# Two early stores moved beside the last row maximum, and six one-element memsets behind it

## The chip, the cores and the metric

The kernel runs on one core of a Trainium2 chip. It uses three engines: SyncE issues the transfers (DMA), VectorE and GpSimd compute. The metric is device time in microseconds (us).

The **span** of a profile goes from the first to the last instruction of the kernel's own program. The **time** is some 1.7 to 2.0 us longer.

## The reference

```python
x = np.random.randn(8192, 8192).astype(np.float32)
return np.linalg.norm(x, ord=np.inf, axis=1)      # the largest |x| of each row
```

It is 268 MB read once and 32 KB written.

## The kernel before

SyncE issues all loads into a ring of buffers (`ring`), VectorE takes the absolute maximum of each piece, and GpSimd combines the maxima of rows that were cut. The first 23 loads of two rows per partition are all alike; the last 18 rows per partition come in 25 loads that get smaller towards the end, so that VectorE and the stream end nearly together. A load waits for its room in the ring, and a maximum waits for the sixteen semaphore increments of its load (the trace of the kernel before has 816 landings, sixteen for each of 48 loads and 3 stores).

```python
def load(self, at, w, src):
    ins = self.nc.sync.dma_start(out=self.ring[:, at : at + w], in_=src)
    ins.then_inc(self.sems[i % SEMS], 16)
    ...
def reduce(self, pairs):
    for k, (dst, src) in enumerate(pairs):
        ins = self.nc.vector.tensor_reduce(out=dst, in_=src, axis=X, op=max, apply_absolute_value=True)
        ...
        ins.wait_op(self.sems[i % SEMS], 16 * (i // SEMS + 1), "sem-ge")     # the first of the load's pieces
    self.last.append(ins.ins)
```

The end of the kernel has three stores: `res_big` (the 46 results per partition of the big loads), the first 16 of the tail's 18 columns, and its last two. SyncE issues the first two right behind the last load; the third waits for the last maximum.

```python
tc.declare_fence(done.ins, group="loads")
nc.sync.dma_start(out=out[:split]..., in_=res_big...)                              # 128 x 184 B
nc.sync.dma_start(out=out_tail[:, : ROWS - 2], in_=res_tail[:, : ROWS - 2])        # 128 x 64 B
seen = nc.sync.keepalive_nop(...)      # waits for GpSimd's last column
last = nc.sync.dma_start(out=out_tail[:, ROWS - 2 :], in_=res_tail[:, ROWS - 2 :]) # 128 x 8 B
```

## Time and profile before

| | before |
|---|---|
| time, median of 3 runs | 629.49 us (629.48 to 629.49) |
| time of the profiled execution | 629.77 us |
| its span | 627.8 us |
| VectorE busy | 551.9 us, 88% |
| DMA, mean | 428 GB/s |

The lines of the page, of the chain, of the timeline and of the traffic that carry the argument stand in the prediction. SyncE's own waits in the last 20 us of the kernel before (who waited, for whom, us in total, times, longest) complete them:

```profile
SPq L218 <- POOL res_tail L202: 13.6, 1, 13.6
SPq L222 <- DVE res_tail L106: 1.3, 1, 1.3
SPq L248 <- DMA out_dram<-res_tail: 1.0, 1, 1.0
```

SyncE has nothing to do from the early stores' issue at 610.5 us to 624.2 us; then it waits for the last maximum, issues the last store, and waits for its landing. So it has room for two issues beside the last maximum.

### The profile page before, as it was taken

The page shows a single profiled execution, that of the slowest core. Times are in us where ns is not written, and L with a number is a line of the kernel's source. Part 1 is how long each engine was busy: PE and PEld are TensorE (multiplying, and loading weights), DVE is VectorE, ACT ScalarE, POOL GpSimd, SP SyncE. Part 2 cuts the span into 40 slices and gives each one's busy share as a digit, 9 for nine tenths or more (in the row PEclk, how much of TensorE's full clock was granted, in tenths as well). Part 3 has the DMA queues.
Part 4 walks back from the last instruction along what each step waited for, and adds up shares of the span by engine and source line. Part 5 has one row for each costly group of instructions (what it writes and reads, how often), then busy time and mean ns, then how long its engine had stood idle before and what let it go on. Part 6 is the DMA issues. An engine that isn't in the chain of part 4 may idle for free.

```text
span 627.8 us, 164 instructions
## 1 busy us (share of the span) xinstructions
DVE 551.9 (88%) x56; POOL 2.9 (0%) x13
## 2 busy tenths in 40 slices
DVE  0588988889988889888898888998889899999998
POOL 0000000000000000000000000000000000000000
DMA  9999999999999999999999999999999999999997
GB/s 401 413 455 409 459 405 463 405 463 401 468 401 468 401 468 401 468 401 468 401 468 401 468 401 468 401 468 401 468 390 435 452 419 438 426 422 431 427 422 284
DMA packets 7344, 268.47 MB, mean 428 GB/s; under 512 B 1200, under 2 KB 1200, under 8 KB 1968
## 3 DMA queue, kind: packets, MB, share of 16 engines
q1 hardware_dynamic: 7344, 268.47, 99.2%
HBM read 268.44 MB, written 0.03 MB: 428 GB/s over the span
## 4 chain that ended last, share of the span: by engine, by line
DMA 59%; DVE 40%; issue 0%; SPq 0%
DMA ring<-in_x_dram 59%; DVE res_big L106 22%; DVE parts L106 10%; DVE res_tail L106 8%; SPq L88 0%
## 5 line engine op out<-in xcount | busy, mean ns | idle before, releaser
L106 DVE TENSOR_REDUCE res_big<-ring 128x2 f32<-128x16384 f32 x23 | 396.1, 17220 | 69.3 <-DMA ring<-in_x_dram 69.3
L106 DVE TENSOR_REDUCE res_tail<-ring 128x1 f32<-128x8192 f32 (+1 forms) x10 | 79.0, 7945 | 2.6 <-DMA ring<-in_x_dram 2.6
L106 DVE TENSOR_REDUCE parts<-ring 128x1 f32<-128x3520 f32 (+17 forms) x19 | 69.8, 3738 | 1.7 <-DMA ring<-in_x_dram 1.7
L106 DVE TENSOR_REDUCE ring<-ring 128x1 f32<-128x1984 f32 (+3 forms) x4 | 7.7, 1982 | 0.0
L202 POOL TENSOR_SCALAR res_tail<-parts 128x1 f32<-128x1 f32 x8 | 2.3, 291 | 614.0 <-DVE parts L106 614.0
L202 POOL TENSOR_SCALAR parts<-parts 128x1 f32<-128x1 f32 x1 | 0.4, 357 | 7.0 <-DVE parts L106 7.0
L237 POOL MEMSET const-bfloat16-1.0<- 128x1 bf16 x1 | 0.1, 103 | 0.0
L237 POOL MEMSET const-uint8-127<- 128x1 uint8 x1 | 0.1, 102 | 0.0
L237 POOL MEMSET const-float32-0.0<- 128x1 f32 x1 | 0.1, 99 | 0.2 <-issue 0.2
L237 POOL MEMSET const-float32-1.0<- 128x1 f32 x1 | 0.1, 99 | 0.0
## 6 DMA issues: line engine op xcount, KB each, us to landing
ring<-in_x_dram SPq DMA_DIRECT2D x3, 4096.0 KB, 41.9
ring<-in_x_dram SPq DMA_DIRECT2D x1, 7488.0 KB, 31.1
ring<-in_x_dram SPq DMA_DIRECT2D x1, 6368.0 KB, 35.4
ring<-in_x_dram SPq DMA_DIRECT2D x1, 5920.0 KB, 40.8
ring<-in_x_dram SPq DMA_DIRECT2D x1, 4800.0 KB, 32.8
ring<-in_x_dram SPq DMA_DIRECT2D x1, 3488.0 KB, 40.4
ring<-in_x_dram SPq DMA_DIRECT2D x1, 3104.0 KB, 39.2
ring<-in_x_dram SPq DMA_DIRECT2D x1, 2944.0 KB, 40.8
```

The lines of the kernel that those rows point to most:

```text
L106: ins = self.nc.vector.tensor_reduce(out=dst, in_=src, axis=mybir.AxisListType.X, op=mybir.AluOpType.max, apply_absolute_value=True,)
L202: combined = nc.gpsimd.tensor_scalar(out=to, in0=best, scalar1=two[0], scalar2=two[1] if len(two) == 2 else None, op0=mybir.AluOpType.max, ...
L237: nc = _bacc.Bacc("TRN2", target_bir_lowering=False, num_devices=1)
```

## The change

Its intent is to keep the small stores out of the DMA queues while the last load lands, and to issue them in the time in which SyncE waits for the last maximum.

```diff
+IDLE = 6
...
+    idle = single.tile([1, IDLE], f32)
...
     tc.declare_fence(done.ins, group="loads")
-    nc.sync.dma_start(
+    for i in range(IDLE):
+        tc.keep_in_program_order(nc.vector.memset(idle[:, i : i + 1], 0.0))
+
+    early = nc.sync.dma_start(
         out=out[:split]..., in_=res_big...
     )
-    nc.sync.dma_start(out=out_tail[:, : ROWS - 2], in_=res_tail[:, : ROWS - 2])
+    middle = nc.sync.dma_start(out=out_tail[:, : ROWS - 2], in_=res_tail[:, : ROWS - 2])
+    for store in (early, middle):
+        tc.add_manual_dep(store.ins, pieces.last[-2].name, ..., reason="not beside the last load")
```

More of the change, by code (lines that the diff above doesn't have):

```diff
@@ L215 @@
     out_tail = out[split:].rearrange("(p r) -> p r", p=P)
-    nc.sync.dma_start(out=out_tail[:, : ROWS - 2], in_=res_tail[:, : ROWS - 2])
+    middle = nc.sync.dma_start(out=out_tail[:, : ROWS - 2], in_=res_tail[:, : ROWS - 2])
+    for store in (early, middle):
+        tc.add_manual_dep(
+            store.ins,
+            pieces.last[-2].name,
+            mybir.DependencyInfo(mybir.DependencyClass.Sync, mybir.DependencyReason.DATA),
+            reason="not beside the last load",
+        )
     seen = nc.sync.keepalive_nop([nc.sync.lower_ap(res_tail[:, ROWS - 2 : ROWS - 1])])
```

## The prediction

> **What bounds the kernel now.** I read the page first, for who is busy; then the chain of work that ended last, for which engine carries the end; then the timeline, the waits and the traffic of the last few microseconds, because the change touches nothing before them.
>
> The head of the page:
>
> ```profile
> span 627.8 us, 164 instructions
> DVE 551.9 (88%) x56; POOL 2.9 (0%) x13
> DMA  9999999999999999999999999999999999999997
> ```
>
> One stream of loads (268 MB at a mean of 428 GB/s) keeps the DMA engines full to the last slice; VectorE follows it, and the tail's loads are cut ever smaller so that VectorE and the stream end nearly together. The change can't touch the 620 us of streaming: it moves two stores that stand behind every load in SyncE's program, and adds instructions behind VectorE's last one. So only the end matters. The chain that ended last, from 600 us on (start, duration, what):
>
> ```profile
> 598.64 10.58 DVE parts L106 x4
> ...
> 609.24 14.89 DMA ring<-in_x_dram
> 624.13 0.02 issue
> 624.15 1.36 DVE res_tail L106
> ```
>
> The end hangs on the landing of the last load, issued at 609.24 and landed at 624.13, and on the last row maximum (128x1156) that waits for it. The timeline shows the wait:
>
> ```profile
> 622.22 1.48 DVE L106 TENSOR_REDUCE parts<-ring 128x1 f32<-128x1280 f32 x1
> 623.87 0.28 POOL L202 TENSOR_SCALAR res_tail<-parts 128x1 f32<-128x1 f32 x1 [8.68 <-DVE parts L106]
> 624.15 1.36 DVE L106 TENSOR_REDUCE res_tail<-ring 128x1 f32<-128x1156 f32 x1 [0.46 <-DMA ring<-in_x_dram]
> 625.54 0.33 SPq L222 DMA_DIRECT2D out_dram<-res_tail  x1
> ```
>
> VectorE ends the last but one maximum at 622.22 + 1.48 = 623.70 and then stands idle for 0.46 us, for the load alone. Was the load's data late? The traffic in windows (window, its length, busy us of DVE and POOL, clock, DMA share, GB/s):
>
> ```profile
> 622.00:622.50 0.50, 0.50 (x2) 0.00 (x0) 1.00 1.03 415
> 622.50:623.30 0.80, 0.80 (x1) 0.00 (x0) 1.00 0.62 172
> 623.30:624.10 0.80, 0.40 (x1) 0.23 (x1) 1.00 0.00 0
> ```
>
> No: from 623.30 to 624.10 nothing moves. The data had come, its completion had not. And this is when the two early stores go through, as their issue-to-landing times say:
>
> ```profile
> out_dram<-res_big SPq DMA_DIRECT2D x1, 23.0 KB, 14.7
> out_dram<-res_tail SPq DMA_DIRECT2D x1, 8.0 KB, 14.4
> out_dram<-res_tail SPq DMA_DIRECT2D x1, 1.0 KB, 1.4
> ```
>
> They were issued at 609.61 and 610.09, right behind the last load, waited in the same queues for its data, and landed at 609.61 + 14.7 = 624.3 and 610.09 + 14.4 = 624.5, on the heels of the last load's landing.
>
> The trace's packet and landing records say how unusual that is. There are 48 loads. For the 41 from the seventh to the last but one, the last of a load's sixteen semaphore landings follows the end of its last data packet by 0.455 to 0.478 us. For the last load it is 1.078 us (data to 623.054, landing at 624.132). The two early stores lag 1.16 and 1.27 us. The last store, alone in the queue, lags 0.40 us. So the last load's completion is some 0.6 us late exactly where 256 packets of 184 and 64 bytes to HBM share the engines with it.
>
> [...] No VectorE memset is in this trace.
>
> **The change, part by part.**
>
> 1. Stores moved. They now wait for the last but one maximum (its semaphore rises at 623.71), so they leave the DMA queues while the last load lands. If they caused its lag, the last load lands at 623.054 + 0.46 = 623.51, which is 0.19 us before the last but one maximum ends. VectorE then is the bound: back to back, a maximum starts 0.09 us before the one before it ends (622.22 against 622.30 at the pair before), so the last one starts at 623.70 - 0.09 = 623.61 instead of 624.15. **Gain 0.54 us** on the path; the last maximum ends at 623.61 + 1.36 = 624.97.
>
> 2. SyncE issues 0.43 us for each of the two stores, with 0.05 us between: from 623.72 to 624.15 and from 624.20 to 624.63. GpSimd's last result, which SyncE also waits for, is there at 624.16. SyncE is free at about 624.7, 0.3 us before the last store may go at 624.98. **Cost 0** on the path, so long as no issue takes much longer.
>
> 3. The last store: issued at 624.98, lands 1.42 us later, at 626.40, if undisturbed. But now the early stores are just ahead of it in the queues. From issue to the first packet the last store took 0.83 us (625.54 to 626.37), so the early ones send packets from about 624.55 and 625.03, and the last one from 625.81. With the lags of 1.16 and 1.27 us that they showed beside the load, the second early store would land at 625.03 + 0.25 + 1.27 = 626.55, behind the last store. Alone in the queue I expect a lag between 0.4 and 1.2 us. **Cost 0 to 0.2 us; I take 0.07.**
>
> 4. Six memsets[...] while SyncE waits for the last store's landing until 626.4. They write a tile that nothing reads. **Cost 0**; I also see no gain, since a maximum's semaphore already rises 12 ns after its end (625.511 to 625.523).
>
> Sum: 629.49 - 0.54 + 0.07 = **629.02 us**, 0.07% less.
>
> **Rivals.**
>
> First, the lag may belong to the stream's end and not to the stores: the last load is the only one with no other load behind it. Then the landing stays at 624.13 and the time at 629.49, or some hundredths above for early stores nearer to the end. [...] against it the 0.40 us of the last store, which has nothing behind it either. I give it 15%.
>
> Second, a new wait: the last store gets stuck behind the two early ones, in SyncE's issue [...], and gives back 0.2 to 0.5 us: 629.15 to 629.45. For it speak the 1.16 and 1.27 us; against it the slack of 0.3 us at SyncE and the stores' spacing of 0.48 us. I give it 20%.
>
> Third, the memsets reach the path, if the end of the program waits for VectorE[...]. Under 3%.
>
> **Range and chances.** Full gain and no cost is 628.95; anything much lower would need a gain from what I count as free, so the low end is 628.84. The first rival sits at 629.49; with its 15% half outside, the high end is 629.45. The repeats of the kernel before lie 0.01 us apart, so the range is of mechanisms and not of noise. Two per cent is 12.6 us, over twenty times all that the change can reach: within 2% is nearly certain.
>
> **What would show each step.** Step 1: VectorE's idle time before the last maximum falls from 0.46 us to nothing, and the last load lands by 623.6. If the idle time stays, the first rival is right. Step 2: SyncE issues the two stores at about 623.7 and 624.2, and the last one within 0.03 us of the last maximum's end. Step 3: the last store takes 1.4 us to landing; 1.6 or more means the second rival, and then the early stores land beside it or after it. [...] The prediction is wrong if the last load still lands late, or if the end waits for an early store.

The sum came to 629.49 - 0.54 + 0.07 = 629.02 us. Step 4's cost of 0 and the 3% of the third rival stand as estimates. The 0.25 us in step 3, for the packets of an early store, is an estimate too; in the changed kernel the packets of the two took 0.25 and 0.20 us from the first to the last.

## The result, and the profile after

The changed kernel took 629.19 us (median of 6 runs, 629.11 to 629.33), the kernel before 629.49 us (median of 6, 629.43 to 629.65). The ratio is 0.9995 (95% interval 0.9982 to 1.0008). Ratios here are the mean time of one kernel's runs over that of the other's of the same rounds, so not quite the ratio of the medians. The ranges of the two don't overlap, and in the five further runs of a control they didn't either (629.15 to 629.27 against 629.42 to 629.74). So 0.3 us is small and repeated, although the stated interval is wider than it. It doesn't show in every single pair: in later rounds on another chip nine runs of the kernel before spread from 629.21 to 630.13 us.

The timeline of the changed kernel's end (start, duration, engine, what) answers to the one in the prediction:

```profile
622.32 1.47 DVE L108 TENSOR_REDUCE parts<-ring 128x1 f32<-128x1280 f32 x1
623.72 1.35 DVE L108 TENSOR_REDUCE res_tail<-ring 128x1 f32<-128x1156 f32 x1
623.82 0.35 SPq L218 DMA_DIRECT2D out_dram<-res_big  x1
623.97 0.28 POOL L205 TENSOR_SCALAR res_tail<-parts 128x1 f32<-128x1 f32 x1 [8.68 <-DVE parts L108]
624.21 0.43 SPq L222 DMA_DIRECT2D out_dram<-res_tail  x1
625.00 0.09 DVE L216 MEMSET idle<- 1x1 f32 x6
625.09 0.33 SPq L235 DMA_DIRECT2D out_dram<-res_tail  x1
```

The last maximum starts at 623.72, before the one ahead of it ends (622.32 + 1.47 = 623.79): the 0.46 us of idle time are gone. The two stores are issued beside it, and the last store leaves at 625.09. The traffic of the changed kernel in the same windows (window, length, busy us of DVE and POOL, clock, DMA share, GB/s):

```profile
622.50:623.30 0.80, 0.80 (x1) 0.00 (x0) 1.00 0.42 167
623.30:624.10 0.80, 0.80 (x2) 0.13 (x1) 1.00 0.04 10
624.10:625.60 1.50, 1.00 (x7) 0.15 (x1) 1.00 0.15 21
```

The early stores' packets now move from 624.67 us on. The 0.04 in the window before is something else: one packet of 8 KB, of a queue that the page of the kernel before doesn't have inside its span. The page of the changed kernel (queue, packets, MB, share) names it:

```profile
q14 instruction: 1, 0.01, 0.0%
```

By the queue's name it is a fetch of instructions. In the kernel before the trace has the same packet too, but at 628.94 us, behind the end of the span at 627.81. It turned out to be half of the story.

One line of the changed kernel misleads. SyncE's waits in the last 20 us:

```profile
SPq L235 <- DVE idle L216: 0.4, 1, 0.4
```

This says that the last store waited for the memsets. The records say otherwise: the last maximum ended at 625.062, the store was issued at 625.089, and the last memset ended at 625.098. The release came from the maximum, 0.027 us after its end, as in the kernel before (625.511 and 625.540, 0.029 us). A wait is put down to the record that fits best in time, and here six memsets lie within 0.1 us of it.

### The profile page after: what moved, and what is told of

It reads as the page before. It is cut to its first block, busy times and chain, and to the rows that moved or that the text cites. A ratio compares the mean times of both kernels' runs of the same rounds, so it can differ in the third digit from the quotient of the medians.

```text
span 627.4 us, 170 instructions
## 1 busy us (share of the span) xinstructions
DVE 551.9 (88%) x62; POOL 2.9 (0%) x13
## 4 chain that ended last, share of the span: by engine, by line
DMA 57%; DVE 42%; issue 0%; DVEq 0%; SPq 0%
DMA ring<-in_x_dram 57%; DVE res_big L108 22%; DVE parts L108 11%; DVE res_tail L108 8%; DVE ring L108 1%; DVEq L261 0%; SPq L90 0%; DVE idle L216 0%
```

## The experiments

The trace's records let the end be cut in two. The first part goes from the start of the last but one maximum to the landing of the last store; the second from there to the end of the time. In the table "lag" is the time from the end of the last load's last data packet to its sixteenth semaphore increment, and "idle" is VectorE's wait before the last maximum (a dash where it started back to back). All are single profiled executions, on several chips; the time is taken to begin with the span.

| kernel | early stores | memsets | lag | idle | first part | second part |
|---|---|---|---|---|---|---|
| before | beside the load | 0 | 1.08 | 0.46 | 4.75 | 2.80 |
| before_look | beside the load | 0 | 0.51 | - | 4.43 | 2.80 |
| before_look2 | beside the load | 0 | 0.68 | 0.09 | 4.35 | 2.80 |
| many_stores_beside | beside the load, more | 6 | 0.65 | 0.07 | 4.34 | 2.67 |
| memsets_only | beside the load | 6 | 0.49 | - | 4.20 | 2.62 |
| stores_only | late | 0 | 0.44 | - | 4.18 | 2.80 |
| after | late | 6 | 0.45 | - | 4.23 | 2.62 |
| after_again | late | 6 | 0.43 | - | 4.19 | 2.63 |
| idle_1 | late | 1 | 0.42 | - | 4.19 | 2.63 |
| memsets_first | late | 6, in front | 0.45 | - | 4.19 | 2.62 |

How to read it: where the stores stand changes the first part alone (medians 4.35 and 4.19 us), and not in every execution; the memsets change the second part alone (2.80 us without them, 2.62 to 2.67 with).

**1. Both parts, once more, as a control.**

> Control: the changed kernel once more, beside its parts on one chip. Every theory: about 0.3 us below the kernel before (629.2 against 629.5), the last maximum back to back behind the one before it, the last load's completion lag 0.45 us.

Measured: 629.20 us (median of 5, 629.15 to 629.27), the kernel before on the same chip 629.57 us (median of 9, 629.42 to 629.74). The difference of 0.37 us repeats the result.

**2. The stores alone.**

```diff
-    for i in range(IDLE):
-        tc.keep_in_program_order(nc.vector.memset(idle[:, i : i + 1], 0.0))
```

> The stores moved, no memsets. Theory 1 (all of the gain is the stores' move; memsets are free): the same as the control within 0.05 us, lag of the last load 0.45 us. Theory 2 (the memsets give part of the gain, because with them an 8 KB instruction fetch that stood at 628.9 us, behind the span, comes at 623.8 us): the span is as the control's, but the time is 0.1 to 0.2 us above it, with the fetch late again. Theory 3 (the memsets cost): 0.05 to 0.1 us below the control.

Measured: 629.49 us (629.37 to 629.60), 0.29 us above the control and only 0.08 us below the kernel before. The end of the span of its profile (627.42 us) is the control's (627.40) within 0.02 us, but the time of that execution is 629.37 against 629.18. So 0.17 us is lost behind the span. The instruction fetch stands at 628.54 us again. The traffic behind the span shows it, in the kernel before, in this one and in the changed kernel (4 GB/s over 2 us are its 8 KB):

```profile
628.00:630.00 2.00, 0.00 (x0) 0.00 (x0) 1.00 0.02 4
628.00:630.00 2.00, 0.00 (x0) 0.00 (x0) 1.00 0.02 4
628.00:630.00 2.00, 0.00 (x0) 0.00 (x0) 1.00 0.00 0
```

Theory 1, which the prediction held, falls; theory 2 has it right, though 0.29 us between the medians is more than its 0.1 to 0.2 (the profiled executions lie 0.19 apart).

**3. The memsets alone.**

```diff
-    for store in (early, middle):
-        tc.add_manual_dep(store.ins, pieces.last[-2].name, ..., reason="not beside the last load")
```

> The six memsets, the stores where they were. Theory 1: the same as the kernel before within 0.05 us, the last load's lag 1.08 us, VectorE idle 0.46 us before the last maximum. Theory 2: 0.1 to 0.2 us below the kernel before, with the instruction fetch at about 623.8 us. Theory 3: up to 0.1 us above it.

Measured: 629.38 us (629.23 to 629.44), 0.19 us below the kernel before (the ranges overlap by 0.02) and 0.18 above the control. The fetch is at 624.30 us. This is theory 2. But the profile showed a second surprise. With the early stores beside the load, VectorE did not wait for it:

```profile
622.57 1.48 DVE L108 TENSOR_REDUCE parts<-ring 128x1 f32<-128x1280 f32 x1
623.96 1.35 DVE L108 TENSOR_REDUCE res_tail<-ring 128x1 f32<-128x1156 f32 x1
```

623.96 lies before 622.57 + 1.48 = 624.05, and the lag is 0.49 us. The 1.08 us that the prediction rests on did not come back. That needed more looks.

**4. Is the lag there in other executions?** The kernel before, unchanged, twice, and one kernel with more stores beside the load.

> A second look at the kernel before. Theory A (the early stores delay the completion of the last load, whatever the run): lag of the last load about 1.08 us again, VectorE idle 0.46 us before the last maximum. Theory B (the lag of the first look was one execution's chance, as the 0.49 us with memsets and early stores hints): lag between 0.45 and 0.8 us, idle time 0 to 0.2 us. Both: the 8 KB instruction fetch at about 628.6 us, behind the span.

Measured: lag 0.51 us, no idle time, time 629.49 us. The two maxima of this look, and its last store in the list of DMA issues (KB, us from issue to landing):

```profile
622.26 1.48 DVE L106 TENSOR_REDUCE parts<-ring 128x1 f32<-128x1280 f32 x1
623.65 1.34 DVE L106 TENSOR_REDUCE res_tail<-ring 128x1 f32<-128x1156 f32 x1
...
out_dram<-res_tail SPq DMA_DIRECT2D x1, 1.0 KB, 1.7
```

Here the last store was slow instead (1.7 us from issue to landing; 1.4 to 1.5 us in the nine other executions of the table), which nothing in the change touches.

> A third look at the kernel before, for how far the last load's completion lag spreads with the early stores beside it. Looks with the stores beside it gave 1.08, 0.51, 0.49 and, with the stores cut small, 0.65 us; those without gave 0.42 to 0.46 us. If the stores delay it by chance: anywhere from 0.47 to 1.1 us, and above 0.46 us again. If they don't: 0.42 to 0.46 us.

Measured: lag 0.68 us, VectorE idle 0.09 us, time 629.60 us.

**5. More small stores beside the load.** The memsets stay; the store of `res_big` is cut into six.

```diff
-    early = nc.sync.dma_start(out=out_big, in_=big)
+    for c in range(0, R * n_big, 8):
+        e = min(c + 8, R * n_big)
+        nc.sync.dma_start(out=out_big[:, c:e], in_=big[:, c:e])
```

> The six memsets, and the early store of 128 packets cut into six of 128 smaller ones, all queued behind the last load: 896 small packets beside its completion instead of 256. Theory A: the lag grows well past that of two stores, to 1.2 us or more, and VectorE waits for the load. Theory B (small stores beside the load don't matter by themselves): lag 0.45 to 0.6 us, last maximum back to back.

Measured: lag 0.65 us, VectorE idle 0.07 us, time 629.26 us. 896 packets instead of 256 did not bring 1.2 us, as theory A wanted it, and the lag is a little past theory B's 0.6. So this look shows no growth of the lag with the number of packets; one look can't exclude it where two stores alone gave 0.49 to 1.08.

Taken together: with stores beside the load the lag was 0.49, 0.51, 0.65, 0.68 and 1.08 us in five executions; without them 0.41 to 0.46 us in seven (the five of the table, and two runs below: 400 memsets, and the smaller last load). The two groups don't overlap, but the gap between them is only 0.03 us, and the lag of ordinary loads differs between executions too (the slowest is 0.478 us in the kernel before and, by the differences below, about 0.50 and 0.45 in its two further looks). The stricter measure is each execution's own loads, from the seventh to the last but one. With the stores beside it, the last load lagged more than the slowest of these in all five executions: by 0.60 us in the kernel before, 0.01 and 0.23 in its two further looks, 0.03 with the memsets alone and 0.20 with more stores. With late stores it never did. So the stores do delay the load's completion, but by 0.01 to 0.60 us, as chance has it, and VectorE waited in three of the five. The first 0.12 us of it cost nothing, since without the stores the load landed 0.12 us before VectorE was ready for it (623.594 against 623.715 in the changed kernel). Why the delay varies so, these runs don't show.

**6. 400 memsets.** To measure what one costs, and the slack behind the last maximum.

```diff
-IDLE = 6
+IDLE = 400
```

> 400 memsets instead of six, which measures the cost of one and the slack behind the last maximum. If one costs what separates two starts in the trace (8 ns), they end 3.2 us after the last maximum at 625.06, thus at 628.3, some 1.6 us past SyncE's last wait at 626.64: time about 630.8 us. If each costs its whole 59 ns, 24 us: about 651 us. If the end of the program doesn't wait for them: as the control.

Measured: 639.39 us (639.30 to 639.54). All three expectations missed. The timeline (start, duration of the group, count, idle time before it):

```profile
625.07 3.11 DVE L216 MEMSET idle<- 1x1 f32 x132
625.16 0.33 SPq L235 DMA_DIRECT2D out_dram<-res_tail  x1
628.51 3.63 DVE L216 MEMSET idle<- 1x1 f32 x128 [0.33 <-issue]
632.46 3.63 DVE L216 MEMSET idle<- 1x1 f32 x128 [0.32 <-issue]
636.42 0.37 DVE L216 MEMSET idle<- 1x1 f32 x12 [0.32 <-issue]
```

The first 40 memsets start mostly 8 to 9 ns apart, the later ones 28 ns apart; why, the run doesn't show. And every 128 memsets VectorE stands still for 0.33 us, waiting for nothing that the profile shows ("issue"). 0.66 us after each of these gaps ends, the trace has one fetch packet of 8192 bytes (629.18, 633.12 and 637.07 us). I read this as blocks of 128 instructions, at whose end VectorE stands still for 0.33 us; no record names such a block. The packet comes after the gap, so the gap is no wait for that packet; what it waits for is not shown. The first block's end lies behind the 132nd memset, so by this reading another lies 128 before it: behind the 4th. This run has a fetch for it too, at 623.81 us.

That would give the memsets their meaning. The records of VectorE's sequencer (DVEq in the profile) run ahead of the engine: in the changed kernel the drain that stands behind the memsets in the program begins at 623.64 us, before the last maximum starts (623.72). So with six memsets it would pass the block's end while VectorE still works at its last maxima: the fetch is at 623.81 us, and the last maximum runs until 625.06. Without them the end would come four instructions past the last maximum. VectorE's records there are a drain, a wait, a drain and a wait, and that wait ends 0.03 us before the span does; so the block would end at the end of the span, where nothing hides it and the time still counts it (0.18 us, below). This is inferred from the fetch 1.13 us behind the span's end in four executions; no record shows VectorE there. The second part of the table is 2.80 us without memsets in four executions and 2.62 to 2.67 with them in the six others of the table: 0.18 us for one memset or six.

**7. One memset.**

```diff
-IDLE = 6
+IDLE = 1
```

> One memset instead of six. In the run with 400 memsets the gaps come behind the 132nd, 260th and 388th, so a block's end lies behind the 4th memset; with one memset it lies three instructions behind it, among the waits of the program's end. Theory 2: no gain or part of it, 629.3 to 629.5 us, and a fetch that comes later than 624.3 us. Rival (one memset keeps VectorE busy as well as six do): 629.2 us with the fetch where six have it.

Measured: 629.16 us (629.11 to 629.36), the kernel before in the same rounds 629.49 us. The time is the full gain, which theory 2 had not expected; but the fetch is at 628.16 us, not at 623.8, which the rival had not expected. I read this as the block's end moving with the number of memsets, by one instruction, ahead of the span's last wait: from the last landing to the end of the span it took 0.975 us instead of 0.845, and the time beyond the span shrank from 1.77 to 1.66 us. The sum of the two, 2.63 us, is that of six memsets. So a fetch behind the span need not cost anything: here it still lies there, 0.62 us behind the end. What counts, by this reading, is where VectorE's pause falls. Its last wait came 0.16 us later than in the control, counted from the drain before it, and the end of the time didn't move. One instruction more was enough here (629.16 us), it seems because the pause falls beside another wait.

**8. The six memsets in front of everything.**

```diff
     idle = single.tile([1, IDLE], f32)
+    for i in range(IDLE):
+        tc.keep_in_program_order(nc.vector.memset(idle[:, i : i + 1], 0.0))
     ...
-    for i in range(IDLE):
-        tc.keep_in_program_order(nc.vector.memset(idle[:, i : i + 1], 0.0))
```

> The changed kernel with the six memsets at the start of VectorE's program. Theory 2 (it is the number of instructions: with six more, VectorE's sequencer passes the end of an 8 KB block of instructions while it waits for the last maximum, not in the program's end): as the changed kernel, 629.2 us, fetch at about 623.5 to 624.3 us. Rival (VectorE must have work behind its last maximum): as the stores alone, 629.5 us, fetch behind the span at 628.5 us.

The 8 KB block of theory 2 is the reading of experiment 6 (gaps 128 memsets apart, packets of 8192 bytes), not a record.

Measured: 629.82 us (629.74 to 629.92), slower than the median of the kernel before (629.49; 629.21 to 630.13). The second part is 2.62 us, so the gain behind the span is there without any work behind the last maximum: the rival falls. Theory 2 has this part right, but missed the time (629.2) and the place of the fetch (623.5 to 624.3). The first load landed 0.39 us later than in the control (22.99 against 22.59 us for the first maximum; the other executions have 22.49 to 22.83), and VectorE's last maximum ended 0.64 us later, of which 0.34 us stand before the tail and 0.30 in it. The timeline of the tail (start, duration, what, idle time before it):

```profile
564.42 13.66 DVE L108 TENSOR_REDUCE parts<-ring 128x1 f32<-128x5888 f32 x3
578.27 3.82 DVE L108 TENSOR_REDUCE parts<-ring 128x1 f32<-128x3520 f32 x1 [0.19 <-DMA ring<-in_x_dram]
```

VectorE waits for a load whose sixteenth increment came at 578.249 us, 0.33 us behind the fifteenth. The instruction fetch was at 574.96 us, of 0.325 us, in the middle of the full stream. That the one delayed the other fits in size and place, but was not tried apart. Nor do the runs tell why the fetch came seventeen maxima earlier rather than six instructions, or what delayed the first load. So the count of instructions is shown to matter (2.80 us in the second part without memsets, 2.62 with six in front), and the exact place of a block's end is not shown.

**9. A smaller last load.** Since the load lands 0.12 us before VectorE is ready for it, the plan might be tightened.

```diff
-FIRST = 1152
+FIRST = 1024
```

> The changed kernel with the last load cut from 1152 to 1024 columns, since its completion now comes 0.12 us before VectorE is ready for it. If the tail can be tightened by that slack: the last maximum is 0.13 us shorter, and the time 629.1 us. If VectorE is the bound through the whole tail, the two loads and maxima that the plan then has more cost some 0.06 us each and eat it up: 629.2 to 629.3 us. If the block's end now falls among the last maxima and stalls VectorE there: 629.4 us or more.

Measured: 629.54 us with a wide range (629.11 to 630.13); before in the same rounds 629.37 us. (The 0.06 us of the expectation is in the changed kernel's trace: its maxima of 1472 and 1280 columns take 1.594 and 1.394 us from one start to the next, thus 1.04 ns a column and 0.06 us besides.) The last maxima of its profile:

```profile
623.02 1.34 DVE L108 TENSOR_REDUCE parts<-ring 128x1 f32<-128x1152 f32 x1
624.28 1.21 DVE L108 TENSOR_REDUCE res_tail<-ring 128x1 f32<-128x1029 f32 x1
```

The last maximum is shorter by 0.13 us, and starts 0.56 us later than in the changed kernel, so VectorE ends 0.43 us later. The new plan has two loads and three maxima more. In the trace, 0.08 us of the 0.43 stand before the tail, 0.20 are a longer wait for loads at the tail's head (4.00 us once, against 2.13 and 1.66), and 0.15 is what the maxima of the tail take more. VectorE doesn't pause behind that wait, so the third expectation's cause is not there; the fetch is at 624.36 us. No version beats the changed kernel; with one memset it is equal.

## Why the prediction was right or wrong

The number was right: 629.02 us predicted, 629.19 measured, inside the range. Two of its four steps were not, and that the number came out was partly luck.

**Step 1, the stores' move: right in mechanism, mis-sized for the median.** What it said of the profile came out: a lag of 0.45 us (0.46 predicted), the landing at 623.594 (623.51), the last maximum back to back. Between the two kept profiles the wait shrank from 0.458 us to an overlap of 0.080, which is 0.54 us, the very term predicted. But the kept profile of before was the worst of the three looks at that kernel. The term that fails is "Gain 0.54 us": the lag of 1.078 us was read as a fixed cost of stores beside a load, and it is a cost that varies between 0.01 and 0.60 us. In the first part of the table, the five executions with the stores beside the load have a median of 4.35 us, and the five with late stores 4.19: 0.16 us. The runs agree: stores alone took 0.08 us off, and with the memsets already there 0.18. These differences are of the size of the runs' spread; the two groups of traces are the better witness. The sign was on the table: the profiled execution took 629.77 us where the median was 629.49, and the sum took the wait of the one from the time of the other. A small misreading stands beside it: the early stores "go through" from 623.30 to 624.10 only in their landings, while their packets moved from 622.54 to 623.22 us, beside the load's last ones.

**Step 2, SyncE's slack: right.** The stores were issued at 623.82 and 624.21 for 0.35 and 0.43 us, and the last one 0.027 us after the last maximum.

**Step 3, the last store behind the early ones: right, and smaller.** It took 1.46 us from issue to landing instead of 1.42; 0.04 us for the predicted 0.07. The other four executions of the table with late stores have 1.41 to 1.43, so no cost is clear of the spread. The early stores' own lags fell from 1.16 and 1.27 us to 0.39 and 0.59 with no load beside them; but the first two are again the worst look, and the three others with these two stores beside the load show 0.56 to 0.73 and 0.65 to 0.82.

**Step 4, the memsets: the cost was right, "I also see no gain" was wrong.** They took 59 ns each, started 2 to 10 ns apart, and ended at 625.10 us, 1.5 us ahead of the last landing. But they gained 0.18 us behind the span, by moving (so the runs point) the end of a block of instructions. The prediction looked at the span alone; the trace of before held the fetch at 628.94 us and the 1.96 us between span and time, and neither was asked about.

The two errors partly cancel: 629.49 - 0.16 for the stores (the 0.04 of step 3 is in that) - 0.18 for the memsets is 629.15 us. That is the luck in the number: the stores brought a third of the 0.47 us forecast for them, and a gain that the prediction had ruled out filled in. The stores alone, which are the prediction's whole mechanism, ran at 629.49 us, on a chip where the kernel before took 629.57.

**The rivals.** The first (the lag belongs to the stream's end) falls: with late stores the lag was never above 0.46 us. The second (the last store gets stuck) falls at 0.04 us or less. The third (memsets on the path) is false for six, and true for 400, which lengthened the time by 10 us.

## What to carry to other kernels

A wait that one profile shows in the last microsecond may be one execution's chance (here 0.46 us in one look, 0 and 0.09 in two more): compare the profiled execution's time with the median, and take two or three more looks before a gain is sized from it. Keep small stores away from the last load that something waits for; what that bought here is an average of a varying delay, 0.16 us between the medians. And when spans are equal and times are not, look behind the span, for instance for instruction fetches: here one instruction more moved the fetch from 1.13 to 0.62 us behind the span's end and took some 0.18 us off the second part of the time. Only memsets were tried as that instruction.
